# One decoder layer on one core: quads for the last depth tiles of the down projection, and helper work placed elsewhere

## The chip, the cores and the metric

The kernel runs on 1 core of one Trainium2 chip. The metric is the device time of one execution in microseconds (us); lower is better. Three runs of the kernel before took 3001.31, 3004.3 and 3009.29 us, median 3004.3.

## The reference

The program is one inference step of a decoder layer in float32, for 2048 prompt positions and 64 sample positions (8 sequences of 8), with a model width of 1024:

```
h     = rms_norm(x, pre_mix_g);  z = h @ w_in           # q, k, v, sg_u, sg_v, mem-q, 3 x 1024 gate logits
attn  = sliding-window attention (128, 8 q heads, 2 kv heads, sinks, rotary)
sg    = gelu(sg_u) * (tril(sg_w) @ layer_norm(gelu(sg_v)) + sg_b)     # chunks of 128
memo  = 4-head attention into 256 memory tokens
mixed = sum over n of sigmoid(gate_n) * (branch_n @ w_o[n])           # 3 branches of width 512
x     = x + rms_norm(mixed, post_mix_g)
up    = rms_norm(x, pre_ffn_g) @ w_up                   # 1024 -> 2 x 2816
c     = causal convolution of width 3 over up, per channel
x     = x + rms_norm((gelu(c_gate) * c_val) @ w_down, post_ffn_g)     # 2816 -> 1024
```

It also returns the new window keys and values, the memory keys and values, the last spatial-gating values and the last two rows of `up`.

## The kernel before

**Tokens and numbers.** All 2112 tokens lie along the free axis, features on the 128 partitions. After the first stage the tokens form three groups of 704 (`T2`), each handled as two halves of 352 columns (`CW`). Float32 operands are split into a high and a low part, the high one by a cast on ScalarE (L76), the low one by a subtraction on VectorE (L77), and each product is three matmuls (`PASSES`).

**Stages.** Stage 1 computes q, k, v, both attentions (pass A), and then the spatial gating (pass B), with a pool of 5 weight buffers `w1`. Then follow the gate phase (three groups of 12 jobs), the mix phase (output projection, gating and the sum of the branches), the up phase (three groups of 22 jobs, with the convolution), and the down phase.

**Seven products instead of eight.** Class `Strassen` (L761) multiplies a pair of output tiles by two halves of a group with seven products. `operands` (L771) loads 8 depth tiles of the activations, scales them where a norm is due (L780), forms four differences (L790) and splits everything into seven operand sets of four tiles (`HK` = 4). `weights` (L813) gives seven weight tiles: three are splits of raw blocks (`r_...`, loaded at L821), four are sums. In the first group of the gate phase the sums are formed on the spot; elsewhere they were formed ahead of time by `prep_sums` (L103), which loads four raw blocks, adds and splits them, and writes them to `sum_d`. A product is 4 depth tiles x 3 passes = 12 matmuls (L882) into a PSUM bank: x (3 of them), y or w (2 each).

**Gate phase.** The x loads `x_h` and their scaling stand at its start, in pool `ldg`.

**Mix phase.** For each group, branch n and pair op, 48 matmuls (L1023) go to two banks; VectorE multiplies by the gate (L1032, L1035), GpSimd adds (L1036). `post_mix` (L988) of a group is called as a whole once the next group has reached n = 0, op = 1: sum of squares over the partitions (L88), reciprocal root (VectorE L92, GpSimd L95), broadcast by an identity matmul (L98), copy, then for eight tiles a scaling (VectorE L1000), an addition of the input (GpSimd L1003), an output and a square.

**Up phase.** `jobs` (L1190) yields the 22 jobs of a group, 84 matmuls each, and calls helpers between them: `prep_sums` for one tile of `w4s` (the down weights) after f = 3, 7, 11, 15, 19 of the first group and f = 3, 7, 11 of the second; `late` (the last group's residual) at f = 2 to 9 of the first group; `norms` of the next group after f = 14. Raw blocks share a pool of 5 (`rawf`), weight tiles one of 11 (`wof`).

**Down phase.** Per group, two blocks of eight depth tiles by `quad` (L1223), four quads each; then the last six depth tiles by `plain` (L1260): 8 output tiles x 2 halves x 18 matmuls (L1279). The squares for the norm are taken in `plain`. `final` (L1295) of a group is called after the first quad of the next group: statistics as above for each half (tile `ps_sd`), eight scalings (L1306), additions of x1 (loads L1304 into two buffers; L1310) and outputs (L1311). The sums y lie in a pool of 10; a group needs 8. In the last group `plain` and `final` run half by half.

**Order.** The kernel is built under `TileContext(nc, schedule_with_timeline_sim=True)`: the program text gives the work and its dependences, and the scheduler sets each engine's order. All loads and stores are issued by one queue, SP, in its order.

Of the kernel before, what the change touches and what calls it, by code (L numbers as in the profile page):

```python
# [15 lines left out]
P = 128  # L16
# [27 lines left out]
def tile_decoder_layer(ctx, tc, I, O):  # L44
# [9 lines left out]
    sum_d = [dpool.tile([4, P, 2, 512], F32, tag=f"sumd{f}", name=f"sum_d{f}") for f in range(NF + 20)]  # L54
# [48 lines left out]
    def prep_sums(rw, wo, w, sums, nm):  # L103


        def block(i):
            t = rw.tile([P, 512], F32, tag="raw", name=f"r{i}_{nm}")
            nc.sync.dma_start(out=t, in_=w[:, i * 512 : (i + 1) * 512])
            return t

        def total(i, p, m, op):
            t = rw.tile([P, 512], F32, tag="raw", name=f"s{i}_{nm}")
            nc.vector.tensor_tensor(out=t, in0=p, in1=m, op=op)
            r = wo.tile([P, 2, 512], F32R, tag="w", name=f"ws{i}_{nm}")
            split(r[:, 0], r[:, 1], t)
            nc.sync.dma_start(out=sums[i], in_=_f(r))
            return t
# [13 lines left out]
def stage1(tc, I, O, br, rbc_d, mhalf, gains, split, PASSES, rstd_rows, ident, ident_r, prep_sums, sum_d):  # L131
    nc = tc.nc
    PSUM = bass.MemoryType.PSUM
    with ExitStack() as c1:
        wp = c1.enter_context(tc.tile_pool(name="w1", bufs=5))
        hp = c1.enter_context(tc.tile_pool(name="h1", bufs=3))
        st = c1.enter_context(tc.tile_pool(name="st1", bufs=3))
        lv = c1.enter_context(tc.tile_pool(name="live1", bufs=2))
        small = c1.enter_context(tc.tile_pool(name="small", bufs=2))
# [4 lines left out]
        def load_w1(u, stage=None, before=None):  # L144
            w = wp.tile([P, 2, KT * 256], F32R, tag="w", name=f"w1_{u}")
# [116 lines left out]
def pass_a(items, a):  # L262
# [42 lines left out]
    w_a = [load_w1(4 + u, stage) for u in range(5)]  # L305
# [440 lines left out]
def stage2(tc, I, O, br, rbc_d, x1_d, acx_d, act_d, sum_d, sg_d, gains, split, PASSES, rstd_rows, prep_sums, m_d, acm_d):  # L746
# [14 lines left out]
    class Strassen:  # L761
# [9 lines left out]
        def operands(self, xs, nm, gain, rb):  # L771
# [21 lines left out]
            J = range(HK)  # L793
# [6 lines left out]
            for j in J:  # L800
                load(j + HK)
                put("b21", j, chunk(x[j + HK], 0))
            for j in J:
                put("t2", j, sub(t[j], chunk(x[j + HK], 1), t[j]))
            for j in J:
                put("b22", j, chunk(x[j + HK], 1))
            for j in J:
                put("t3", j, sub(chunk(x[j], 1), chunk(x[j + HK], 1), chunk(x[j], 1)))
            for j in J:
                put("t4", j, sub(t[j], chunk(x[j + HK], 0), t[j]))  # L810
            return ops

        def weights(self, w, sums, first, nm):  # L813

            _, _, wo, rw, _, _ = self.pools
            raw = {}

            def block(i):
                if i not in raw:
                    raw[i] = rw.tile([P, HK * P], F32, tag="raw", name=f"r{i}_{nm}")  # L820
                    nc.sync.dma_start(out=raw[i], in_=w[:, i * 512 : (i + 1) * 512])  # L821
# [51 lines left out]
        def product(self, q, bank, w, o, start):  # L873
# [5 lines left out]
            ps, n = banks[bank], 0  # L879
            for j in range(HK):  # L880
                for a, b in PASSES:
                    nc.tensor.matmul(  # L882
                        ps[:, :CW], lhsT=ws[w][:, a, j], rhs=ops[o][j][:, b],
                        start=(start and n == 0), stop=(n == 3 * HK - 1), skip_group_check=True,
# [19 lines left out]
def gate_phase(c2, tc, env):  # L904
# [42 lines left out]
def mix_phase(c2, tc, env):  # L947
# [12 lines left out]
    bc, sp, wp, gp, me = (pool(c2, nm, n) for nm, n in (("bc", 4), ("s2", 2), ("w2", 3), ("sg2", 5), ("mxe", 8)))  # L960
# [510 lines left out]
```

## Time and profile before

| | |
|---|---|
| median of three runs | 3004.3 us |
| profiled execution, its span | 3005.72 us, 3003.9 us |
| mean granted TensorE clock | 0.977 |
| TensorE busy | 2876.0 us, 96% of the span, 19340 instructions |
| VectorE busy | 2064.8 us, 69% |
| ScalarE, GpSimd busy | 1397.5 us (47%), 488.3 us (16%) |
| DMA queue q1 | 728.97 MB, 69.9% of 16 engines |

Busy time is given per engine; the span is the time from the first to the last instruction. The granted clock is the share of full speed that TensorE had, 1.00 for 2.4 GHz. A wait in the profile is the idle time of an engine just before an instruction, with the instruction or transfer that ended it.

### The profile page before, as it was taken

How to read it: one execution, taken by the hardware profiler on the slowest of the kernel's cores; microseconds unless marked ns; L12 is line 12 of the kernel's file. 1: busy time of each engine (PE TensorE's matmuls, PEld its weight loads, DVE VectorE, ACT ScalarE, POOL GpSimd, SP SyncE). 2: the span in 40 equal slices, each digit the busy share in tenths (PEclk: the TensorE clock that was granted, in tenths of full speed). 3: DMA queues.
4: the chain of work that ended last, by engine and by line, in shares of the span. 5: the costliest groups of instructions: out<-in, count | busy, mean ns of one | idle time of the engine just before them, and what ended most of it. 6: DMA issues, size and time to landing. Idle time of an engine off the chain costs nothing. (4 is left out here: it accounts for less than half of the span.)

```text
span 3003.9 us, 52626 instructions
## 1 busy us (share of the span) xinstructions
PE 2876.0 (96%) x19340; PEld 2829.2 (94%) x19340; DVE 2064.8 (69%) x3901; ACT 1397.5 (47%) x2799; POOL 488.3 (16%) x576
## 2 busy tenths in 40 slices
PE   8999999996999999999999899999999999999996
PEld 8998999996999999999989899999999999999996
DVE  6676567888867363478798677766775667667665
ACT  5555557333555353432235355644554454343332
POOL 3221100010000000035453121311231121000000
PEclk9999999998999999999999899999999999999998
DMA  6222224787989999867669788887777778576673
GB/s 209 53 69 85 76 68 126 258 303 248 328 296 371 332 356 346 320 212 264 212 249 364 291 304 310 319 288 278 246 277 247 240 238 279 196 273 223 233 246 119
DMA packets 310946, 732.33 MB, mean 244 GB/s; under 512 B 37968, under 2 KB 90192, under 8 KB 310672
## 3 DMA queue, kind: packets, MB, share of 16 engines
q1 hardware_dynamic: 310688, 728.97, 69.9%
q8 instruction: 153, 2.51, 0.3%
q14 instruction: 105, 0.86, 0.1%
HBM read 553.55 MB, written 176.27 MB: 243 GB/s over the span
## 5 line engine op out<-in xcount | busy, mean ns | idle before, releaser
L1023 PE MATMUL ps_p<-b,w_p 128*128 128x352 f32 x1728 | 287.2, 328 | 13.3 <-DVE m L1032 8.8
L1023 PEld LDWEIGHTS ps_p<-b,w_p 128*128 128x128 f32 x1728 | 283.3, 192 | 15.1 <-issue 10.2
L1165 DVE SCALAR_TENSOR_TENSOR c<-e,k_conv_w,c 128x704 f32<-128x704 f32 (+1 forms) x264 | 251.6, 954 | 43.3 <-ACT c L1161 36.0
L882 PE MATMUL ps_xu<-ot_u,ws_u 128*128 128x352 f32 x1584 | 274.9, 322 | 0.0
L882 PEld LDWEIGHTS ps_xu<-ot_u,ws_u 128*128 128x128 f32 x1584 | 257.1, 188 | 0.0
L1036 POOL TENSOR_TENSOR m<-m,sl 128x704 f32<-128x704 f32 x48 | 101.4, 2119 | 658.0 <-DVE sl L1035 651.8
L77 DVE TENSOR_TENSOR wa_u<-r_u,wa_u 128x512 fp32r<-128x512 f32 x198 | 138.6, 703 | 48.0 <-ACT wa_u L76 43.9
L1161 ACT ACTIVATE c<-e,k_conv_b,k_conv_w 128x704 f32<-128x704 f32 (+1 forms) x132 | 129.6, 981 | 78.6 <-DVE e L1140 43.5
L882 PE MATMUL ps_xu<-ob_u,wa_u 128*128 128x352 f32 x792 | 149.0, 325 | 9.7 <-ACT wa_u L76 9.7
L1152 POOL COPY tails<-e 128x2 f32<-128x2 f32 x88 | 79.2, 900 | 470.0 <-DVE e L1140 469.6
L882 PE MATMUL ps_xg<-ot_h,ws_g 128*128 128x352 f32 x864 | 151.1, 323 | 1.7 <-ACT ws_g L76 0.8
L882 PE MATMUL ps_wu<-ob_u,wa_u 128*128 128x352 f32 x792 | 147.0, 324 | 1.1 <-DVE ob_u L77 1.1
L882 PE MATMUL ps_yu<-ot_u,ws_u 128*128 128x352 f32 x792 | 143.2, 325 | 3.8 <-DVE sl L1035 2.2
L76 ACT CAST wa_u<-r_u 128x512 fp32r<-128x512 f32 x198 | 123.1, 623 | 47.1 <-PE ps_xu L882 15.7
L882 PEld LDWEIGHTS ps_xg<-ot_h,ws_g 128*128 128x128 f32 x864 | 140.6, 188 | 2.4 <-ACT ws_g L76 1.3
L882 PEld LDWEIGHTS ps_xu<-ob_u,wa_u 128*128 128x128 f32 x792 | 131.7, 190 | 9.9 <-ACT wa_u L76 9.9
L1279 PE MATMUL ps_p<-a,wd 128*128 128x352 f32 x864 | 140.1, 323 | 0.0
L1279 PEld LDWEIGHTS ps_p<-a,wd 128*128 128x128 f32 x864 | 138.4, 188 | 0.1
L882 PE MATMUL ps_xu<-ot_u,wa_u 128*128 128x352 f32 x792 | 138.0, 323 | 0.0
L882 PE MATMUL ps_yu<-ob_u,ws_u 128*128 128x352 f32 x792 | 137.7, 323 | 0.0
L882 PEld LDWEIGHTS ps_yu<-ot_u,ws_u 128*128 128x128 f32 x792 | 130.9, 190 | 4.6 <-DVE sl L1035 2.5
L1140 DVE TENSOR_TENSOR e<-p_u,ps_wu 128x352 f32<-128x352 f32 x66 | 34.3, 519 | 145.1 <-PE ps_wu L882 140.3
(381 smaller groups left out, 6786.2 us busy)
## 6 DMA issues: line engine op xcount, KB each, us to landing
ws_u<-sum_d SPq DMA_DIRECT2D x264, 512.0 KB, 4.9
r_u<-in_w_dram SPq DMA_DIRECT2D x286, 256.0 KB, 4.7
ws_g<-sum_d SPq DMA_DIRECT2D x96, 512.0 KB, 8.5
ws_d<-sum_d SPq DMA_DIRECT2D x96, 512.0 KB, 5.1
sum_d<-ws_u SPq DMA_DIRECT2D x88, 512.0 KB, 4.2
r_g<-in_wg_dram SPq DMA_DIRECT2D x120, 256.0 KB, 5.3
r_d<-in_w4s_dram SPq DMA_DIRECT2D x104, 256.0 KB, 4.4
sg_d<-sg SPq DMA_DIRECT2D x72, 352.0 KB, 5.0
```

The source lines that it names most:

```text
L76: nc.scalar.copy(out=hi, in_=src)
L77: nc.vector.tensor_tensor(out=lo, in0=src, in1=_f(hi), op=ALU.subtract)
L882: nc.tensor.matmul(ps[:, :CW], lhsT=ws[w][:, a, j], rhs=ops[o][j][:, b], start=(start and n == 0), stop=(n == 3 * HK - 1), skip_group_chec ...
L1023: nc.tensor.matmul(ps[:, c, :CW], lhsT=w[:, a, 4 * oo + k], rhs=bs[k][:, b, c * CW : (c + 1) * CW], start=(i == 0), stop=(i == 11),)
L1036: nc.gpsimd.tensor_tensor(out=mx[o], in0=mx[o], in1=sg, op=ALU.add)
L1140: lambda out, part: nc.vector.tensor_tensor(out=out, in0=part(p), in1=part(q), op=ALU.add), h, c
L1152: nc.gpsimd.tensor_copy(out=tails[:, ft], in_=e[:, T2 : T2 + 2])
L1161: nc.scalar.activation(c[:, :cwid], e[:, 2:ew], AF.Identity, bias=cb[:, ft : ft + 1], scale=cw[:, ft, 2:3])
L1165: nc.vector.scalar_tensor_tensor(out=c[:, :cwid], in0=e[:, t : t + cwid], scalar=cw[:, ft, t : t + 1], in1=c[:, :cwid], op0=ALU.mult, op1= ...
L1279: nc.tensor.matmul(ps[:, :CW], lhsT=w[k // 4][:, a, k % 4], rhs=acts[k][c][:, b], start=(n == 0), stop=(n == 3 * ND - 1),)
```

## The change

1. **Down phase.** A third block of quads with three depth tiles in each half (`hk` = 3) replaces `plain` in the first two groups. Its weights come from a new input `w4t`, 384 columns to a block, and their sums from four more `prep_sums` (`wide` = 384). Squares are taken in the third block (`done`), and a quad's last product runs into the next group's first quad. The last group is as before.
2. **Up phase.** `prep_sums` is called twelve times, after f = 11 and 14 of the first group, 2, 5, 8, 11, 14 of the second and 1, 4, 7, 10, 13 of the third. `norms` stands after f = 18. `wof` has 10 buffers.
3. **Stage 1 and gate phase.** The pool `w1` has 4 buffers, and one weight of pass A has a buffer of its own. In pass B a tile `free1b` keeps a place of the size of `ldg` free, so that the gate phase's x sources can be loaded and scaled early. The gate and mix pools are opened in another order.
4. **Mix phase.** `post_mix` is a generator: the statistics, then two output tiles at a step, one step after each (n, op) of the next group.
5. **`final`.** The x1 loads have 4 buffers, in the last group 8 in the pool `ldf`.

```diff
@@ prep_sums
-    def prep_sums(rw, wo, w, sums, nm):
+    def prep_sums(rw, wo, w, sums, nm, wide=512):
...
-            nc.sync.dma_start(out=t, in_=w[:, i * 512 : (i + 1) * 512])
-            return t
+            nc.sync.dma_start(out=t[:, :wide], in_=w[:, i * wide : (i + 1) * wide])
+            return t[:, :wide]
@@ stage1
-        wp = c1.enter_context(tc.tile_pool(name="w1", bufs=5))
+        wp = c1.enter_context(tc.tile_pool(name="w1", bufs=4))
...
+            wx = c2.enter_context(tc.tile_pool(name="w1x", bufs=1, side="right"))
...
+            free = c2.enter_context(tc.tile_pool(name="free1b", bufs=1, side="right", reuse_waits="tile"))
+            free.tile([P, 11 * T2], F32, tag="free", name="free1b")
@@ Strassen.product
-            for j in range(HK):
+            for j in range(hk):
@@ mix_phase, post_mix
         acx = xp.tile([P, T2], F32, tag="ax", name=f"acx_{g}")
+        yield
         for o in range(KT):
...
             square(acx, m, o == 0, f"x{g}_{o}")
+            if o % 2:
+                yield
...
-                if held and n == 0 and op == 1:
-                    post_mix(*held)
-                    held = None
-        held = g, mx, acc
+                if held and (n, op) > (0, 0):
+                    next(held, None)
+        held = post_mix(g, mx, acc)
@@ up_phase, jobs
+        preps = [(g, f) for g, fs in ((0, (11, 14)), (1, (2, 5, 8, 11, 14)), (2, (1, 4, 7, 10, 13))) for f in fs]
...
-                if f % 4 == 3 and 5 * g + f // 4 < 8:
-                    i = 5 * g + f // 4
-                    prep_sums(rw, wo, I["w4s"][i], sum_d[NF + 12 + i], f"d{i}")
+                if (g, f) in preps:
+                    i = preps.index((g, f))
+                    w = I["w4s"][i] if i < 8 else I["w4t"][i - 8]
+                    prep_sums(rw, wo, w, sum_d[NF + 12 + i], f"d{i}", 512 if i < 8 else 384)
...
-                if f == 14 and g + 1 < NG2:
+                if f == 18 and g + 1 < NG2:
@@ down_phase
+        done(0)
         add(1, 1, eng.product(q, "x", "s3", "t3", False))
-        return lambda: put(1, 0, eng.product(q, "x", "a22", "t4", False))
+
+        def last():
+            put(1, 0, eng.product(q, "x", "a22", "t4", False))
+            done(1)
+
+        return last
...
-            x = sp.tile([P, T2], F32, tag="x", name=f"xf_{g}_{o}_{c0}", bufs=2)
+            if g + 1 == NG2:
+                x = lp.tile([P, T2], F32, tag="ld", name=f"xf_{g}_{o}_{c0}", bufs=8)
+            else:
+                x = sp.tile([P, T2], F32, tag="x", name=f"xf_{g}_{o}_{c0}", bufs=4)
...
-        for b in range(NB):
-            ops = eng.operands(lambda k: act_d[8 * b + k][:, g * T2 : (g + 1) * T2], f"d{g}_{b}", None, None)
+        for b in range(NB + (g + 1 < NG2)):
+            hk = (HK, HK, ND // 2)[b]
+            ops = eng.operands(
+                lambda k: act_d[8 * b + k][:, g * T2 : (g + 1) * T2], f"d{g}_{b}", None, None, hk
+            )
...
+                end = quad(nm, ws, ops, two, b == 0, end, *((done,) if b == NB else ()))
                 if held:
                     final(*held)
                     held = None
+                    acc = sp.tile([P, T2], F32, tag="acc", name=f"acc_{g}", bufs=1)
-        acts = load_acts(g)
...
         if g + 1 < NG2:
-            plain(g, acts, ys, (0, 1), acc, end)
-            held, end = (g, ys, acc, (0, 1)), None
+            held = g, ys, acc, (0, 1)
```

**Where the order moves, 1: TensorE in the first group of the up phase.** `ps_su_1` is the second half's statistics for the next group's norm; `ps_xu_7` is a bank of job 7. Before:

```order
L882 MATMUL ps_xu_7_18938<-ot_u_3_17844,wa_u_7_18931 128x352 x3
L88 MATMUL ps_su_1_20133<-ones,acx_20118 88x1 x4
L98 MATMUL ps_su_1_20133<-ident,rstd_u_1_20138 128x88 x4
L882 MATMUL ps_xu_8_19118<-ob_u_0_17722,wa_u_8_19093 128x352 x2
L882 MATMUL ps_wu_8_19170<-ob_u_0_17766,wa_u_8_19100 128x352 x2
```

Now:

```order
L88 MATMUL ps_su_1_20670<-ones,acx_20655 88x1 x4
L885 MATMUL ps_xu_19_20708<-ob_u_0_17735,wa_u_19_20683 128x352 x3
L885 MATMUL ps_xu_18_20540<-ot_u_0_17829,ws_u_18_20531 128x352 x3
...
L885 MATMUL ps_yu_19_20745<-ot_u_2_17768,ws_u_19_20688 128x352 x3
L885 MATMUL ps_yu_19_20745<-ot_u_3_17773,ws_u_19_20688 128x352 x2
L98 MATMUL ps_su_1_20670<-ident,rstd_u_1_20675 128x88 x4
```

The pair has moved from between jobs 7 and 8 to jobs 18 and 19, and 35 matmuls (the rows left out are eight of three) stand between its two parts.

**2: VectorE behind `post_mix`'s statistics of the first group.** `rs` is the broadcast root, `m_0` to `m_7` are the eight tiles that are scaled; the `m_5` with `ps_p_0_5` is a product of the next group. Before:

```order
L1032 TENSOR_TENSOR m_4_16037<-sl_0_4_16035,ps_p_0_4_16010 128x704
L994 COPY rs_15939<-ps_st_15919 128x704
L1000 SCALAR_TENSOR_TENSOR m_0_14986<-m_0_14986,c_gains,rs_15939 128x704
...
L1000 SCALAR_TENSOR_TENSOR m_7_15204<-m_7_15204,c_gains,rs_15939 128x704
L1032 TENSOR_TENSOR m_5_16066<-sl_0_5_16064,ps_p_0_5_16039 128x704
```

Now:

```order
L1038 TENSOR_TENSOR m_4_15987<-sl_0_4_15985,ps_p_0_4_15960 128x704
L997 COPY rs_15952<-ps_st_15932 128x704
L1004 SCALAR_TENSOR_TENSOR m_0_14999<-m_0_14999,c_gains,rs_15952 128x704
...
L1004 SCALAR_TENSOR_TENSOR m_7_15217<-m_7_15217,c_gains,rs_15952 128x704
L1038 TENSOR_TENSOR m_5_16016<-sl_0_5_16014,ps_p_0_5_15989 128x704
```

Nothing has moved: the scalings of `m_1` to `m_6` are the rows left out in both.

**3: TensorE at the start of the second down group.** `ps_sd_1` is the statistics of the first group's second half; `ps_xd_0_1`, `ps_wd_0_2` and `ps_xd_0_3` are banks of the second group's quads 1, 2 and 3. Before:

```order
L98 MATMUL ps_sd_1_29761<-ident,rstd_d_1_29766 128x88 x4
L882 MATMUL ps_yd_0_2_29985<-ot_d_0_2_29553,ws_d_0_2_29940 128x352 x2
L882 MATMUL ps_yd_0_2_29985<-ot_d_0_3_29558,ws_d_0_2_29940 128x352 x3
L882 MATMUL ps_wd_0_2_29999<-ob_d_0_0_29563,wa_d_0_2_29942 128x352 x3
...
L882 MATMUL ps_xd_0_3_30077<-ob_d_0_3_29538,wa_d_0_3_30054 128x352 x3
L882 MATMUL ps_xd_0_1_29839<-ot_d_0_0_29582,ws_d_0_1_29828 128x352 x3
```

Now:

```order
L885 MATMUL ps_xd_0_3_30245<-ob_d_0_3_29692,wa_d_0_3_30222 128x352 x3
L88 MATMUL ps_sd_1_29928<-ones,acc_28007 88x1 x4
L98 MATMUL ps_sd_1_29928<-ident,rstd_d_1_29933 128x88 x4
L885 MATMUL ps_xd_0_1_30007<-ot_d_0_0_29736,ws_d_0_1_29996 128x352 x3
L885 MATMUL ps_xd_0_1_30007<-ot_d_0_1_29740,ws_d_0_1_29996 128x352 x3
```

The products of `ps_wd_0_2` and `ps_xd_0_3`, which stood behind L98, now stand ahead of L88, and L98 follows L88 directly.

## Rows read from the trace of the kernel before

**Rows 1.** The page's parts 1 and 5: busy time, share; a group's busy time, mean ns.

```profile
PE 2876.0 (96%) x19340; PEld 2829.2 (94%) x19340; DVE 2064.8 (69%) x3901; ACT 1397.5 (47%) x2799; POOL 488.3 (16%) x576
...
L1279 PE MATMUL ps_p<-a,wd 128*128 128x352 f32 x864 | 140.1, 323 | 0.0
```

**Rows 2.** What TensorE waits for: us in total, times, longest.

```profile
PE ps_xg L882 <- ACT wa_g L76: 19.1, 2, 17.0
PE ps_xd L882 <- ACT y L1229: 17.5, 3, 6.8
PE ps_xu L882 <- ACT wa_u L76: 9.7, 1, 9.7
PE ps_p L1023 <- DVE m L1032: 8.8, 2, 4.4
```

**Rows 3.** Windows of 50 us: busy us and instructions per engine, granted clock, DMA.

```profile
1650.00:1700.00 50.00, 36.32 (x216) 35.51 (x215) 40.72 (x62) 17.68 (x30) 11.73 (x13) 0.81 0.77 283
1700.00:1750.00 50.00, 50.00 (x307) 49.76 (x307) 31.05 (x46) 24.72 (x44) 10.37 (x14) 0.98 0.82 292
2600.00:2650.00 50.00, 50.00 (x314) 50.00 (x313) 37.61 (x76) 22.93 (x46) 0.00 (x0) 1.00 0.57 191
```

**Rows 4.** Timeline of the up phase: start, us, instruction, idle before.

```profile
1683.90 6.12 DVE L780 SCALAR_TENSOR_TENSOR x_u<-x_u,c_gains,rb 128x704 f32<-128x704 f32 x7
1684.38 7.03 SPq L821 DMA_DIRECT2D r_u<-in_w_dram  x3
...
1690.37 0.69 DVE L113 TENSOR_TENSOR s_d<-r_d,s_d 128x512 f32<-128x512 f32 x1
...
1692.28 0.95 PE L882 MATMUL ps_xu<-ob_u,wa_u 128*128 128x352 f32 x2 [9.66 <-ACT wa_u L76]
```

**Rows 5.** Timeline of post_mix of the first group.

```profile
1371.73 12.81 DVE L1000 SCALAR_TENSOR_TENSOR m<-m,c_gains,rs 128x704 f32<-128x704 f32 x8
...
1385.48 14.75 PE L1023 MATMUL ps_p<-b,w_p 128*128 128x352 f32 x75 [4.44 <-DVE m L1032]
```

**Rows 6.** Timeline at the start of the gate phase.

```profile
723.58 1.06 PE L732 MATMUL psg<-sgwb,vg 128*128 128x128 f32 x8
...
737.35 1.82 DVE L77 TENSOR_TENSOR ob_h<-x_h,ob_h 128x352 fp32r<-128x352 f32 x4
...
744.14 1.50 SPq L821 DMA_DIRECT2D r_g<-in_wg_dram  x3
...
748.80 0.95 PE L882 MATMUL ps_xg<-ob_h,wa_g 128*128 128x352 f32 x2 [16.95 <-ACT wa_g L76]
```

**Rows 7.** Timeline at the start of the second down group.

```profile
2660.87 0.71 PE L88 MATMUL ps_sd<-ones,acc 128*88 128x1 f32 x8
...
2661.93 1.00 POOL L95 TENSOR_TENSOR rstd_d<-rstd_d,mhalf 88x4 f32<-88x4 f32 x1 [7.14 <-DVE rstd_d L92]
...
2665.86 1.02 PE L98 MATMUL ps_sd<-ident,rstd_d 88*128 88x88 f32 x8
...
2677.86 0.45 ACT L1229 COPY y<-ps_xd 128x352 f32<-128x352 f32 x1 [5.77 <-DMA out_yT_dram<-y]
...
2678.36 3.48 PE L882 MATMUL ps_xd<-ot_d,ws_d 128*128 128x352 f32 x12 [6.80 <-ACT y L1229]
```

**Rows 8.** Timeline of the end: scalings alone, and with GpSimd beside them.

```profile
2961.41 4.06 DVE L1306 SCALAR_TENSOR_TENSOR y<-y,c_gains,rs_d 128x352 f32<-128x352 f32 x8
...
2982.24 4.72 DVE L1306 SCALAR_TENSOR_TENSOR y<-y,c_gains,rs_d 128x352 f32<-128x352 f32 x8
2983.40 1.20 POOL L1310 TENSOR_TENSOR y<-y,xf 128x352 f32<-128x352 f32 x1 [3.82 <-DVE y L1306]
...
2986.89 1.11 DVE L1310 TENSOR_TENSOR y<-y,xf 128x352 f32<-128x352 f32 x2
...
2996.25 0.94 DVE L1310 TENSOR_TENSOR y<-y,xf 128x352 f32<-128x352 f32 x1 [3.52 <-DMA xf<-x_d]
...
3001.20 0.33 SPq L1311 DMA_DIRECT2D out_yT_dram<-y  x1
```

More of the change, by code (lines that the diff above doesn't have):

```diff
@@ L53, in tile_decoder_layer @@
     acx_d = [dpool.tile([P, T2], F32, tag=f"acxd{g}", name=f"acx_d{g}") for g in range(NG2)]
-    sum_d = [dpool.tile([4, P, 2, 512], F32, tag=f"sumd{f}", name=f"sum_d{f}") for f in range(NF + 20)]
+    sum_d = [dpool.tile([4, P, 2, 512], F32, tag=f"sumd{f}", name=f"sum_d{f}") for f in range(NF + 24)]
     sg_d = [dpool.tile([P, NTOK], F32, tag=f"sgd{i}", name=f"sg_d{i}") for i in range(24)]
@@ L142, in stage1, with load_w1 @@
         ps_tr = c1.enter_context(tc.tile_pool(name="ps_tr", bufs=2, space=PSUM))
-        def load_w1(u, stage=None, before=None):
-            w = wp.tile([P, 2, KT * 256], F32R, tag="w", name=f"w1_{u}")
+        def load_w1(u, stage=None, before=None, pool=None):
+            w = (pool or wp).tile([P, 2, KT * 256], F32R, tag="w", name=f"w1_{u}")
             for i in range(2):
@@ L304, in pass_a @@
     rb_mem, r_mem = rstd_of(x_mem, NMEM, "mem")
-    w_a = [load_w1(4 + u, stage) for u in range(5)]
+    w_a = [load_w1(4 + u, stage, pool=None if u else a["wx"]) for u in range(5)]
     band = kload("band", [P, 256])
@@ L769, in __init__, with operands @@
             self.pools = ps, op_, wo, rw, cp, lp
-        def operands(self, xs, nm, gain, rb):
+        def operands(self, xs, nm, gain, rb, hk=HK):
             _, op_, _, _, _, lp = self.pools
@@ L791, in sub @@
                 return out
-            J = range(HK)
+            J = range(hk)
             for j in J:
@@ L883, in product @@
                         ps[:, :CW], lhsT=ws[w][:, a, j], rhs=ops[o][j][:, b],
-                        start=(start and n == 0), stop=(n == 3 * HK - 1), skip_group_check=True,
+                        start=(start and n == 0), stop=(n == 3 * hk - 1), skip_group_check=True,
                     )
@@ L1051, in ffn_phase @@
     env["lp"], env["rw"], env["wo"] = (
-        pool(c2, nm, n, "right") for nm, n in (("ldf", 1), ("rawf", 5), ("wof", 11))
+        pool(c2, nm, n, "right") for nm, n in (("ldf", 1), ("rawf", 5), ("wof", 10))
     )
@@ L1221, in down_phase, with quad @@
     eng = Strassen(ps2, op_, wo, rw, None, lp)
-    def quad(nm, ws, ops, ys, first, end):
+    def quad(nm, ws, ops, ys, first, end, done=lambda o: None):
         q = [nm, ws, ops, None, {}]
@@ L1287, in plain @@
                 nc.vector.tensor_tensor(out=chunk(ys[o], c), in0=chunk(ys[o], c), in1=ps[:, :CW], op=ALU.add)
[L1288 to L1293 removed]
+            squares(acc, ys[o], o, c0, c1, nm)
     def final(g, ys, acc, cs):
@@ L1320, in down_phase, with done @@
                     ys += [yp.tile([P, T2], F32, tag="y", name=f"y_{g}_{2 * op + h}") for h in range(2)]
-                i, nm = 4 * b + op, f"d{g}_{b}_{op}"
-                ws = eng.weights(I["w4s"][i], sum_d[NF + 12 + i], False, nm)
-                end = quad(nm, ws, ops, ys[2 * op : 2 * op + 2], b == 0, end)
+                i, nm, two = 4 * b + op, f"d{g}_{b}_{op}", ys[2 * op : 2 * op + 2]
+                ws = eng.weights(I["w4s"][i] if b < NB else I["w4t"][op], sum_d[NF + 12 + i], False, nm, hk)
+                def done(o, op=op, two=two, acc=acc, nm=nm):
+                    squares(acc, two[o], 2 * op + o, 0, T2, f"{nm}_{o}")
+                end = quad(nm, ws, ops, two, b == 0, end, *((done,) if b == NB else ()))
                 if held:
@@ L1411, in _layout @@
     )
+    r["w4t"] = np.stack(
+        [
+            np.concatenate([dn[2 * op + oo][:, 16:].reshape(P, (NF - 16) * P) for oo in range(2)], 1)
+            for op in range(4)
+        ]
+    )
     r["w4"] = np.stack([dn[o][:, 16:].reshape(P, (NF - 16) * P) for o in range(KT)])
```

60 lines of the change are left out of this document (31 added, 29 removed).

## The prediction

> **What bounds the kernel now.** I read the page first, then the list of what TensorE waits for, then 50-us windows, and then the timeline around each long wait. TensorE is busy for 2876.0 of 3003.9 us [rows 1], so it is the bound almost everywhere, and a change is worth either the matmuls that it removes or the idle stretches that it closes; a faster helper engine alone brings nothing. A stretch without waits holds 314 matmuls of 352 columns in 50 us, 0.16 us each, at a granted clock of 1.00, which is the 2.4 GHz level (the window from 2600 us) [rows 3]. The idle stretches are few. The largest single one, 17.0 us, stands ahead of the gate phase; three before ps_xd sum to 17.5, one in the up phase is 9.7, and two before ps_p are 4.4 each [rows 2]. Each costs more than its idle time, because the matmuls behind it run slower: the 12 behind the 6.80 us wait took 3.48 us instead of 1.92 [rows 7], and the window of the up-phase wait has a granted clock of 0.81, a mixture of the two levels, 1.2 and 2.4 GHz [rows 3]. At the very end TensorE is done while VectorE, GpSimd and the queue still work for 20 us [rows 8].
>
> **The change part by part.** Each part is set against the profiled execution, 3005.72 us, 1.4 us above the median of 3004.3.
>
> *Fewer matmuls.* The plain product of the last six depth tiles is 864 matmuls, 288 per group [rows 1]. In two groups it becomes four quads of 7 products x 3 depth tiles x 3 passes = 63, so 252. That is 2 x 36 = 72 matmuls less, x 0.16 = **-11.5 us**. They lie on TensorE's path with no wait around them [rows 3], so this is a full gain, if the quads keep pace.
>
> *Do they keep pace?* Plain, VectorE is busy 37.61 of 50 us [rows 3], or 34.7 us over a group's 46.1 us of matmuls. In the quads the next group's operands are the same; from the code I count 32 additions into y instead of 16, and 12 narrower weight splits instead of 16, at about half a microsecond each, some 5 us more, and 40.3 us of matmuls: 39.7 of 40.3. Every add or split that comes late holds a PSUM bank or a weight. I take +2 us per group, **+4 us**, with 0 and +8 as the ends.
>
> *Up phase, first group.* The two statistics of the next group's norm stand back to back, and with them come seven scalings in a row (6.12 us), in front of the sums of a w4s tile (s_d at 1690.37). The raw-weight buffers are held by those sums, so the queue takes 7.03 us to issue three r_u loads, and TensorE waits 9.66 us for wa_u [rows 4]. Moving norms from f = 14 to f = 18, and the sums to f = 11 and 14, takes both away from each other: in the new order 35 matmuls, 5.6 us, stand between L88 and L98 of the second statistics, and from L88 to the end of the step on GpSimd the same chain took 2.06 us in the down phase [rows 7]; three weights ahead are already split when the scalings begin, and no sums are near. The two windows hold 216 and 307 matmuls against 314 [rows 3], so (98 + 7) x 0.16 = **-16.8 us** is there to be had. The eight scalings and four subtractions, some 9 us of VectorE, now hide behind the matmuls of a job, 84 x 0.16 = 13.4 us. If that cover fails, the stall comes back: the term lies between -16.8 and 0. I take all of it. The four new sums in the second and third group land in windows where VectorE has a third of its time free; I cost them at nothing, and at 4 us if they meet the scalings.
>
> *post_mix stepped.* VectorE runs the eight scalings in 12.81 us, and TensorE waits 4.44 us behind them, twice, and then runs 75 matmuls in 14.75 instead of 12.0 [rows 5]. The generator should spread them. But the scheduler has set them in the same place as before: copy, eight scalings, then the product's m_5, in both groups. I cost it at **0**; -14, both stalls with their slow matmuls, is out of reach in that order, and a shift of some loads behind the scalings may move it by 2 either way.
>
> *Early gate sources.* The first group's x_h loads and scalings go to the start of pass B. What TensorE waits for is wa_g, cast from r_g, and r_g is issued at 744.14 [rows 6]. In the new order the r_g loads stand behind a load of the second group's first x_h, whose buffer comes free with the first t3 split. From the end of the psg matmuls at 724.6 I count 29 VectorE instructions of 352 columns up to that split, 0.455 each [rows 6], and 11 of 512, 0.69 each [rows 4]: 20.8 us, so 745, the same within 1 us. **0**, from -6 (had the queue gone on) to +4 (a second weight then split later).
>
> *Boundaries between the down groups.* The second group's y_2 needs the buffer of the first group's y_0, which is free once its output is written: TensorE's next product waits 6.80 us [rows 7]. This stays. The chain from L88 at 2660.87 to the restart at 2678.36 is 17.49 us, and before it has 9 us of matmuls inside (56 x 0.16). In the new order these are all issued ahead: L88, L98 and then the waiting product, nothing between. L98 need no longer queue behind other matmuls (POOL is done at 2662.93, L98 ran at 2665.86), which shortens the chain by 2.9 us to 14.6; 1.7 of it is L88 and L98, and 12.9 is idle against 6.8. With 1.4 us more at the low clock, +7.5 per boundary, twice: **+15 us**, from 0 (if TensorE arrives there late anyway) to +20.
>
> *The last group's x1 loads.* At the end, additions wait for loads that wait for buffers, two by two: from the scalings at 2982.24 to the last output at 3001.20 is 18.96 us [rows 8]. With eight buffers all loads are issued before the scalings start. Left are the scalings, four additions on VectorE at 0.55 (two took 1.11) and the issue, 0.4. Eight scalings took 4.06 us alone and 4.72 with one GpSimd addition beside them [rows 8]; with three beside, 4.06 + 3 x 0.66 = 6.0. So 6.0 + 2.2 + 0.4 = 8.6, a gain of **-10.4 us**, from -12.5 (no disturbance) to -4 (some loads still late). The Trainium skill, "SBUF — State Buffer", section "SBUF: two separate sides", speaks against more than that: VectorE with two SBUF inputs and GpSimd take the shared port pair in turn, each for a whole instruction. By that rule the three additions, 1.20 each [rows 8], would cost in full, 7.7 instead of 6.0, and the term would be -8.7; the row at 2982.24 shows half of it, so I stay with the row.
>
> *Fourth w1 buffer less, one wof buffer less.* A weight of the up phase has 9 products or more, 17 us, from its buffer's release to its use. 0, with 4 either way at the start of pass B.
>
> Sum: -11.5 + 4 - 16.8 + 0 + 0 + 15 - 10.4 = -19.7, so 3005.7 - 19.7 = 2986.0, or 2984.6 against the median. I say **2985 us**.
>
> **The rivals.** A difference under 0.3%, 9 us, can't be told from none here: 2995 to 3013.
>
> *A, the boundaries cost nothing new.* For it: TensorE loses the same chain either way if VectorE's additions and splits, 39.7 of 40.3 us, make it arrive late. Against it: the new order has nothing behind L98. Then 2984.6 - 15 - 4 = 2965.6. Chance 0.12.
>
> *B, the up-phase stall moves and does not go.* For it: all eight scalings still stand in a row, and wa_u of jobs 20 and 21 stand behind them. Against it: they are needed a job later. Then 2984.6 + 16.8 = 3001, the same. Chance 0.16.
>
> *C, slower: the narrow quads starve on VectorE.* One place, the two third blocks; mechanism: at 39.7 of 40.3 us every wait is handed on to the next bank, and TensorE between such waits drops to the low level, where 12 matmuls took 3.48 us (0.29 each), 0.13 more than before. With half of the 504 matmuls there, 252 x 0.13 = 33 us, 3017. It decides from about 14 us lost per group on; there the whole forecast gain and 9 us more are gone. Against it: with the plain product VectorE is at three quarters of its time and TensorE waits nowhere [rows 3], and part of the operands' subtractions can be done a block earlier. Chance 0.07.
>
> *D, the forecast,* stepping and early sources without effect: 0.65, own range 2972 to 2995.
>
> **How the numbers follow.** Faster: A, D except the few cases past 2995 (0.04 of 0.65), so 0.12 + 0.61 = 0.73. Same: B and those few, 0.20 with rounding. Slower: C, 0.07. The range goes from 2969, in the middle of A, to 3001, B's own number: outside lie half of A, C and a part of B's upper half, near 0.2.
>
> **What would show it.** ps_p's group with the last six depth tiles has 288 matmuls left, all in the last group. No wait near the tenth job of the up phase. The two 4.4 us waits behind post_mix's scalings stand as before, and so does the wait ahead of the gate phase, 15 to 19 us. Two waits of ps_xd behind y's copy of 12 to 14 us, in place of 6.8. From the last scalings to the last output 8 to 9 us. The forecast is wrong if the boundary waits are near 7, if the up stall returns at jobs 19 to 21, or if TensorE shows many short waits for VectorE in the third blocks.

## The result, and the profile after

The changed kernel took 2981.5 us (median of four runs, 2978.1 to 2983.4), the kernel before 3002.8 beside it: a ratio of 0.9924 (95% interval 0.9908 to 0.9940), 21 us less. 2985 had been said. The profiled execution took 2978.08 us, span 2976.3, 27.6 less than the profiled one of before; since both lie off their medians, on opposite sides, some 6 us of that is scatter.

Where the 27.6 us lie, by the first and last matmuls of each stage's products in the two timelines (the tail holds the last statistics, too):

| stretch | before | after | difference | forecast |
|---|---|---|---|---|
| start to the gate's first product | 748.8 | 737.6 | -11.2 | 0 |
| gate phase | 505.1 | 509.8 | +4.7 | 0 |
| mix, to the first up product | 307.7 | 304.5 | -3.2 | 0 |
| up phase | 927.3 | 917.0 | -10.3 | -16.8 |
| down, last up product to last down product | 485.6 | 488.3 | +2.7 | +7.5 |
| tail, to the end of the span | 29.4 | 19.2 | -10.2 | -10.4 |

What TensorE waits for now (us in total, times, longest), against [rows 2]:

```profile
PE ps_xd L885 <- ACT y L1236: 24.0, 3, 11.5
PE ps_xg L885 <- ACT wa_g L76: 19.9, 2, 18.2
PE ps_p L1029 <- DVE m L1038: 9.1, 2, 4.6
...
PE psg L735 <- DVE ob L739: 5.9, 1, 5.9
PE ps_sd L98 <- POOL rstd_d L95: 5.1, 3, 1.8
```

The up phase's wait for wa_u is gone; the two before post_mix's products stand unchanged, the one ahead of the gate phase is 1.3 longer, and ps_xd's has grown. Windows of 50 us (PE, PEld, DVE, ACT, POOL, then granted clock, DMA share, GB/s), against [rows 3]:

```profile
1650.00:1700.00 50.00, 50.00 (x317) 49.99 (x317) 33.57 (x48) 24.68 (x42) 11.63 (x17) 1.00 0.89 330
1800.00:1850.00 50.00, 50.00 (x321) 49.99 (x320) 41.53 (x65) 25.30 (x47) 11.94 (x17) 1.00 0.70 235
2150.00:2200.00 50.00, 46.70 (x289) 45.85 (x288) 47.37 (x90) 31.21 (x62) 31.14 (x23) 1.00 0.79 282
2650.00:2700.00 50.00, 41.09 (x246) 41.09 (x247) 38.91 (x73) 19.81 (x44) 0.00 (x0) 0.87 0.82 304
2750.00:2800.00 50.00, 50.00 (x314) 50.00 (x313) 44.31 (x91) 23.87 (x47) 0.00 (x0) 1.00 0.90 301
```

At 1650 us there are 317 matmuls in place of 216, and at 1800 us, where the next group's scalings now stand, 321. At 2150 us, where the third up group begins and a preparation of sums stands after its second job, there are 289, where its neighbours hold 312 to 316; two waits stand there:

```profile
2189.84 0.59 PE L885 MATMUL ps_wu<-ob_u,wa_u 128*128 128x352 f32 x2 [1.35 <-ACT wa_u L76]
...
2193.44 2.16 PE L885 MATMUL ps_yu<-ot_u,ws_u 128*128 128x352 f32 x12 [1.41 <-DMA ws_u<-sum_d]
```

At 2750 us, in a third block of quads, VectorE is at 44 of 50 and TensorE waits for nothing: the quads keep pace. At 2650 us lies a boundary between down groups; its timeline (start, us, instruction, idle before), against [rows 7]:

```profile
2643.75 0.71 PE L88 MATMUL ps_sd<-ones,acc 128*88 128x1 f32 x8
...
2646.29 1.12 PE L98 MATMUL ps_sd<-ident,rstd_d 88*128 88x88 f32 x8 [1.82 <-POOL rstd_d L95]
...
2648.01 6.99 DVE L1325 SCALAR_TENSOR_TENSOR y<-y,c_gains,rs_d 128x704 f32<-128x704 f32 x8
2654.91 3.29 DVE L1329 TENSOR_TENSOR y<-y,xf 128x704 f32<-128x704 f32 x4
2655.83 0.34 SPq L1330 DMA_DIRECT2D out_yT_dram<-y  x1
...
2658.40 0.45 ACT L1236 COPY y<-ps_xd 128x352 f32<-128x352 f32 x1 [13.45 <-DMA out_yT_dram<-y]
...
2658.91 3.89 PE L885 MATMUL ps_xd<-ot_d,ws_d 128*128 128x352 f32 x12 [11.50 <-ACT y L1236]
```

TensorE stands for 1.82 + 11.50 = 13.3 us, and most of that is VectorE: y_0 is scaled first, but its addition stands behind all eight scalings (6.99 us). The end, against [rows 8]:

```profile
2964.26 6.06 DVE L1325 SCALAR_TENSOR_TENSOR y<-y,c_gains,rs_d 128x352 f32<-128x352 f32 x8
2965.42 1.20 POOL L1329 TENSOR_TENSOR y<-y,xf 128x352 f32<-128x352 f32 x1 [3.82 <-DVE y L1325]
2966.65 7.10 SPq L1330 DMA_DIRECT2D out_yT_dram<-y  x8
...
2970.25 2.55 DVE L1329 TENSOR_TENSOR y<-y,xf 128x352 f32<-128x352 f32 x4
```

No wait for a load is left, and the last output is issued within 9.5 us of the first scaling. Mix and gate, against [rows 5, 6]:

```profile
732.91 0.33 SPq L781 DMA_DIRECT2D x_h<-in_xT_dram  x1
...
733.30 1.37 SPq L824 DMA_DIRECT2D r_g<-in_wg_dram  x3
...
737.64 0.95 PE L885 MATMUL ps_xg<-ob_h,wa_g 128*128 128x352 f32 x2 [18.21 <-ACT wa_g L76]
...
1366.03 12.78 DVE L1004 SCALAR_TENSOR_TENSOR m<-m,c_gains,rs 128x704 f32<-128x704 f32 x8
...
1379.75 2.69 PE L1029 MATMUL ps_p<-b,w_p 128*128 128x352 f32 x8 [4.52 <-DVE m L1038]
```

The weights r_g leave right behind the second group's x_h, as the order had it, and the scalings are as long as before (12.81).

### The profile page after: what moved, and what is told of

The parts are those of the page before. It is cut to its first block, busy times and chain, and to the rows that moved or that the text cites. A ratio compares the mean times of both kernels' runs of the same rounds, so it can differ in the third digit from the quotient of the medians.

```text
span 2976.3 us, 52703 instructions
## 1 busy us (share of the span) xinstructions
PE 2856.3 (96%) x19268; PEld 2808.2 (94%) x19268; DVE 2096.1 (70%) x3991; ACT 1408.1 (47%) x2819; POOL 502.6 (17%) x576
## 4 chain that ended last, share of the span: by engine, by line
PE 85%; DVE 5%; DMA 5%; issue 2%; ACT 2%; POOL 1%; SPq 0%; DVEq 0%; ACTq 0%; POOLq 0%
PE ps_xu L885 17%; PE ps_xg L885 9%; PE ps_yu L885 8%; PE ps_p L1029 8%; PE ps_xd L885 8%; PE ps_yg L885 5%; PE ps_wu L885 4%; PE ps_yd L885 4%; PE ps_mqp L229 3%; PE ps_q L215 3%; PE ps_wg L885 2%; PE ps_wd L885 2%; PE ps_kv L215 2%; PE ps_sv L215 2%; PE ps_up L229 1%
## 5 line engine op out<-in xcount | busy, mean ns | idle before, releaser
L885 PE MATMUL ps_xd<-ot_d,ws_d 128*128 128x352 f32 x720 | 129.4, 329 | 24.0 <-ACT y L1236 24.0
L1157 POOL COPY tails<-e 128x2 f32<-128x2 f32 x88 | 73.2, 832 | 460.4 <-DVE e L1145 450.3
L885 PEld LDWEIGHTS ps_xd<-ot_d,ws_d 128*128 128x128 f32 x720 | 120.0, 193 | 24.7 <-ACT y L1236 24.7
L885 PEld LDWEIGHTS ps_wu<-ob_u,wa_u 128*128 128x128 f32 x792 | 131.3, 190 | 1.9 <-ACT wa_u L76 1.9
```

The costliest lines, as they stand in the source:

```text
L885: nc.tensor.matmul(ps[:, :CW], lhsT=ws[w][:, a, j], rhs=ops[o][j][:, b], start=(start and n == 0), stop=(n == 3 * hk - 1), skip_group_chec ...
L1157: nc.gpsimd.tensor_copy(out=tails[:, ft], in_=e[:, T2 : T2 + 2])
```

## Experiments

Twelve kernels ran, each with the kernel before on the same chip (medians 3003.7 to 3005.4 us).

| kernel | median us (lowest to highest) | ratio to before, 95% interval |
|---|---|---|
| changed, old places in the up phase | 3000.9 (2996.9 to 3007.1) | 0.9992 [0.9984, 1.0001] |
| changed, old stage 1 and gate | 2982.7 (2978.2 to 2986.2) | 0.9930 [0.9918, 0.9942] |
| changed, plain product | 2981.8 (2974.2 to 2985.8) | 0.9926 [0.9914, 0.9938] |
| changed, old x1 buffers | 2994.4 (2988.6 to 2996.4) | 0.9966 [0.9954, 0.9979] |
| 12 y buffers | 2962.6 (2961.3 to 2968.2) | 0.9869 [0.9854, 0.9883] |
| 12 y buffers, plain | 2960.5 (2958.0 to 2962.8) | 0.9858 [0.9843, 0.9873] |
| 12 y buffers, scalings held apart | 2966.9 (2964.0 to 2975.6) | 0.9882 [0.9867, 0.9897] |
| 12 y buffers, f = 12, 13 in the gate | 2955.4 (2949.9 to 2957.5) | 0.9836 [0.9823, 0.9849] |
| new placement, plain | 2933.0 (2925.0 to 2935.2) | 0.9756 [0.9742, 0.9771] |
| new placement, quads, 15 y buffers | **2924.3** (2923.5 to 2927.9) | 0.9735 [0.9721, 0.9748] |
| the same, additions on GpSimd | 2939.8 (2936.8 to 2945.5) | 0.9790 [0.9777, 0.9804] |
| the same, two more sums moved | 2941.1 (2936.0 to 2942.6) | 0.9781 [0.9767, 0.9795] |

### Parts undone

**Up phase.**

```diff
-((0, (11, 14)), (1, (2, 5, 8, 11, 14)), (2, (1, 4, 7, 10, 13)))
+((0, (3, 7, 11, 15, 19)), (1, (3, 7, 11, 15, 19)), (2, (3, 7)))
-                if f == 18 and g + 1 < NG2:
+                if f == 14 and g + 1 < NG2:
```

> The changed kernel with the up phase's part undone: norms after f = 14 again, and the twelve preparations of sums in the old raster, after f = 3, 7, 11, 15, 19. The changed kernel stands at 2981.5 us. Theory of the prediction: the 9.7 us wait near the tenth job of the first up group comes back whole with its slow matmuls, +16.8, 2998. Second theory, from the two traces: from the first to the last up matmul only 10.3 us went, because the five preparations of the third group take some back (two waits of 1.4 us at its second job); then the stall comes back and those waits go, +10, 2992. Rival: other parts of the change took the stall away (buffers, order), so nothing comes back, 2980 to 2984.

The first theory's number came (2998 said, 3000.9 measured), and its wait, in the timeline of this kernel:

```profile
1691.28 0.95 PE L885 MATMUL ps_xu<-ob_u,wa_u 128*128 128x352 f32 x2 [12.38 <-ACT wa_u L76]
```

But of the 19.4 us only 15.0 lie in the up phase (932.0 against 917.0); the down phase, whose order changed too, takes 5.6 more. Split at every 1848 matmuls, the up phase shows where (us per group of tokens):

| kernel | first group | second | third |
|---|---|---|---|
| before | 324.7 | 299.1 | 303.5 |
| changed | 309.1 | 299.3 | 308.6 |
| changed, old places | 329.8 | 299.1 | 303.1 |

The stall was worth 15.6 us, near the 16.8 said. What hides it in the total is the third group, 5.1 longer in the changed kernel. It is not the number of sums: in the old raster the second and third groups have two more each than before and take no longer, and the changed kernel's second group has five for three; a kernel further down has six in the third group and takes 303.1. What the changed kernel's third group alone has is a sum after its second job, f = 1, with the two short waits shown above. The first group of this kernel is 5.1 longer than before's with the same five sums; one weight buffer less and the order are not told apart there.

**Stage 1 and gate.** The gate and mix pools are opened in the old order too.

```diff
-        wp = c1.enter_context(tc.tile_pool(name="w1", bufs=4))
+        wp = c1.enter_context(tc.tile_pool(name="w1", bufs=5))
...
-            wx = c2.enter_context(tc.tile_pool(name="w1x", bufs=1, side="right"))
...
-            free.tile([P, 11 * T2], F32, tag="free", name="free1b")
```

> The changed kernel with stage 1's and the gate phase's part undone: w1 has 5 buffers, no extra weight buffer, no place kept free for early sources, gate and mix pools in the old order. Theory: the 12.4 us by which the last psg matmuls came earlier (717.35 instead of 729.77) are this part's work, although I had put it at 0; undone, psg ends near 730 again, of which the gate phase gives 4.7 back, so +6.5, 2988, and up to 2992. Rival: the 12.4 us are scatter between two executions (granted clock at the start of pass B); then psg ends at 717 to 720 here too, and the time stays at 2979 to 2984.

Mixed. The last psg matmuls end at 729.8 here, against 719.4, and between 717 and 724 in the six other runs with the same pass B: the gain is this part's work, no scatter. Some 6 of the 10.4 us are there at the first psg matmuls already (531.7 against 525.8). In the pass the short waits for h_bp are back. But the medians differ by 1.2 us only, inside the runs' spread; by the two profiled executions 4.6 reach the end of the up phase. What the part is worth, 1 to 5, stays open.

**Plain product for the quads.**

```diff
-        for b in range(NB + (g + 1 < NG2)):
+        for b in range(NB):
...
+            plain(g, acts, ys, (0, 1), acc, end)
+            held, end = (g, ys, acc, (0, 1)), None
```

> The changed kernel with the plain product of the last six depth tiles in all three groups again; the other parts stay, the four added preparations too. 72 matmuls come back, +11.5. Theory, from the traces: the two boundaries fall back from 13.3 us of idle time to about 6.8, with fewer slow matmuls behind them, -13 to -15, so the quads as they stand bring nothing: 2979, between 2976 and 2982. Prediction's terms taken alone (11.5 - 4 - 15 = -7.5): 2974. Rival: the boundary waits don't come from the quads and stay at 13 us; then +11.5, 2993.

As the traces' theory said: 2981.8, so in the changed kernel 72 fewer matmuls bring nothing. Each of its boundaries has 5.3 us of wait for wa_d and 1.0 for y, in place of 13.3.

**x1 buffers.**

```diff
-            if g + 1 == NG2:
-                x = lp.tile([P, T2], F32, tag="ld", name=f"xf_{g}_{o}_{c0}", bufs=8)
-            else:
-                x = sp.tile([P, T2], F32, tag="x", name=f"xf_{g}_{o}_{c0}", bufs=4)
+            x = sp.tile([P, T2], F32, tag="x", name=f"xf_{g}_{o}_{c0}", bufs=2)
```

> The changed kernel with the x1 loads of final as before: two buffers in every group. Theory (the term of the prediction): from the last eight scalings to the last output 19 us again instead of 9, so +10.4, 2992; the boundary waits of the first two groups stay at 11.5, since y_0's output doesn't need a third load. Rival: with eight loads in flight at the end the additions still wait, and the whole gain at the end came from the shorter statistics: then +3, 2984.

+12.9 by the medians; the scalings start at 2970.86 and the last output is issued at 2989.34, 18.5 us. The theory holds, 2.5 us stronger.

### The boundary

```diff
-    yp, sp = pool(c2, "yd", 10), pool(c2, "sd", 1)
+    yp, sp = pool(c2, "yd", 12), pool(c2, "sd", 1)
...
-                x = sp.tile([P, T2], F32, tag="x", name=f"xf_{g}_{o}_{c0}", bufs=4)
+                x = sp.tile([P, T2], F32, tag="x", name=f"xf_{g}_{o}_{c0}", bufs=2)
```

> The changed kernel with 12 instead of 10 buffers for y in the down phase, paid for with 2 instead of 4 buffers for the x1 loads of the first two groups. Theory: the wait at a boundary is for the buffer of y_0 alone; with two more buffers the second quad of a group (13.4 us of matmuls) runs while the first outputs leave, so both waits of 11.5 us go, and their slow matmuls: -2 x 12.5, 2957, between 2954 and 2962. Rival: the wait moves on to the third quad, because with two x1 buffers the outputs of y_0 and y_1 leave later than 13 us after L88: half comes back, 2969. Second rival: TensorE is held by L98's wait for GpSimd (1.8 us) and by VectorE anyway, and only a third goes: 2973.

-18.9 of the -25 said. At the first boundary of this kernel the waits are shorter and later:

```profile
2660.75 0.43 PE L885 MATMUL ps_xd<-ob_d,wa_d 128*128 128x352 f32 x1 [1.64 <-DVE ob_d L77]
...
2664.55 3.89 PE L885 MATMUL ps_xd<-ot_d,ws_d 128*128 128x352 f32 x12 [3.37 <-ACT y L1236]
```

So it lies between theory and first rival: the wait moved on to the third quad and shrank.

**With the plain product** in addition, by the same edit as above:

> The kernel with 12 buffers for y (2962.6 us), with the plain product of the last six depth tiles in all three groups. It tells what the quads are worth once no buffer of y holds the boundary. Theory: 72 matmuls x 0.16 = +11.5, and the plain form's boundary had its own wait for y and a weight (5.3 us), which goes with the buffers too: 2974, between 2971 and 2977. Rival 1: the quads are worth nothing even then (their additions keep VectorE as late as the matmuls saved): 2963. Rival 2: with plain, the two buffers bring nothing, since its statistics had more matmuls beside them: 2982.

My theory failed: plain is not 11.5 us slower (2.2 faster, with overlapping ranges). With 12 buffers the plain form has no wait beyond 0.6 us at a boundary, the quads keep 2 x (3.4 + 1.6) and slow matmuls: that still eats the 72.

### Work around the waits

**Scalings held apart.** `post_mix` scales into a tile of its own with two buffers.

```diff
+            s = xp.tile([P, T2], F32, tag="sm", name=f"sm_{g}_{o}", bufs=2)
...
-            nc.gpsimd.tensor_tensor(out=m, in0=m, in1=x, op=ALU.add)
+            nc.gpsimd.tensor_tensor(out=m, in0=s, in1=x, op=ALU.add)
```

> The kernel with 12 buffers for y (2962.6 us), and post_mix's scaling writes to a tile of its own with two buffers, which GpSimd's addition frees; so the scheduler can't set eight scalings in a row any more: in the order two stand ahead of m_5, two behind it, and the rest one by one between products. Theory: the two waits of 4.5 us for m_5 go, with the slow matmuls behind them, -14 as worked out before the run: 2949, between 2947 and 2955. Rival: the scalings themselves were not the wait; VectorE is short by the same time spread over the next jobs, and half comes back: 2956.

Refuted. Both waits for m_5 are gone, yet the up phase starts only 0.7 us earlier. TensorE ran ahead and then stood in a window where VectorE has no time left (columns as above, this kernel first, then the one with the scalings in a row):

```profile
1500.00:1550.00 50.00, 42.64 (x253) 41.26 (x252) 48.02 (x54) 13.97 (x22) 26.24 (x12) 0.97 0.60 209
```

```profile
1500.00:1550.00 50.00, 46.97 (x294) 46.11 (x294) 48.04 (x54) 16.18 (x25) 28.69 (x13) 1.00 0.63 224
```

As I read it, the stall was the price of VectorE work due anyway before the up phase's first operands. The +4.3 in the total lies in the down phase (477.1 against 471.8), whose order differs too.

**Two sums out of pass B.**

```diff
-NF1 = 14
+NF1 = 12
...
-                if g and i % 3 == 0:
+                if g and i % 5 in (0, 2):
```

> The kernel with 12 buffers for y (2962.6 us), with the sums of two up weights (f = 12 and 13) formed in the gate phase instead of at the end of pass B. In the order the gate's first weight loads then stand right behind the last of these stores, ahead of pass B's last two outputs, and all r_g of the first two jobs are split before x_h is done. Theory: the 18 us wait ahead of the gate phase was for VectorE's and the queue's work on f = 12 and 13 (16 VectorE instructions of 0.69, 11 us, and eight stores), not for the x sources; it falls to 5 or less, -13 with the slow matmuls behind it, 2950. Rival: the first products then wait for the x_h splits, 28 VectorE instructions, as long as before: 2961. The ten sums in the gate phase cost under 2 us there.

The theory on the start holds: the gate's first product comes at 717.3 instead of 737.1, with 1.75 us of wait. But the gate phase ends only 8.5 earlier, and 7.2 of the 13 us said came in all; from 900 us on TensorE waits for weights (wa_g, 8.7 us) and for ScalarE's copies of products (u_g, 9.0), with the DMA nearly full:

```profile
900.00:950.00 50.00, 48.75 (x302) 48.17 (x301) 24.21 (x41) 18.54 (x36) 0.00 (x0) 1.00 1.00 381
...
1100.00:1150.00 50.00, 43.44 (x250) 42.25 (x249) 19.95 (x33) 20.66 (x40) 0.00 (x0) 0.93 0.98 360
```

That the DMA is the cause is not shown: without these two sums the first window holds 312 matmuls at a DMA share of 0.99.

### Put together

The sums of f = 12 and 13 are formed in the gate phase, f = 20 and 21 in the first up group; the sums of the down weights follow from the second group on, after f = 2, 5, 8, 11, 14 and, in the third, 4, 8, 12. The down phase is plain, with 12 y buffers.

```diff
-NF1 = 14
+NF1 = 12
...
-        todo = list(range(NF1, NF))
+        todo = list(range(NF1, NF - 2))
...
+                if g == 0 and f in (11, 14):
+                    f1 = NF - 2 + (f == 14)
+                    prep_sums(rw, wo, I["w3"][f1], sum_d[f1], f"u{f1}")
```

> A version put together from the runs: plain last six depth tiles in all groups, 12 buffers for y, the sums of f = 12 and 13 in the gate phase, those of f = 20 and 21 in the first up group (after f = 11 and 14), so the gate phase has its eight sums as before, and only the eight sums of w4s in the up phase. Theory: 2960.5 (plain with 12 buffers) - 7.2 for the gate start - 3 for the two sums that the gate's DMA (0.9 to 1.0 busy from 900 us on) need not carry - 4.7 for the four sums of w4t that are not formed (the up phase with twelve in the old raster was 4.7 longer than with eight): 2946, between 2942 and 2952. Rival: the sums cost nothing where they stand, only the gate start counts: 2953.

13 us better than said: the gate phase takes 506.8 us here against 521.6 with ten sums, so two sums there, and the closer places of all ten, cost 15, not 3. The gate's first group, which has no sums, takes as long in both (170.8 and 169.8). The up phase's third group, without a sum after f = 1, is back at 303.1, so the theory's 4.7 came for that place and not for four sums fewer.

**With the quads,** so with four more sums, after f = 1, 4, 7, 10, 13, 16 of the second group and 2, 5, 8, 11, 14, 17 of the third:

```diff
-    yp, sp = pool(c2, "yd", 10), pool(c2, "sd", 1)
+    yp, sp = pool(c2, "yd", 15), pool(c2, "sd", 1)
...
-                x = sp.tile([P, T2], F32, tag="x", name=f"xf_{g}_{o}_{c0}", bufs=4)
+            x = lp.tile([P, T2], F32, tag="ld", name=f"xf_{g}_{o}_{c0}", bufs=8)
```

> The same placement of sums, with the quads of three depth tiles in the first two groups (so twelve sums in the up phase), and 15 buffers for y, which take the place of final's own x1 and root buffers (these come from the operands' load pool). Theory: the quads lost their 11.5 us to the last y waits (2 x 3.4, and slow matmuls behind them) and to VectorE being late at the boundary (2 x 1.6); with 15 buffers the y waits go, and the quads are worth about 8 over plain, less 4.7 for the four sums: 2943. Rival: VectorE is the limit at the boundary (eight scalings and eight additions of 0.87, 14 us, beside a block's operands), and the waits only change their name to ob_d and wa_d: as plain or slower, 2947 to 2955.

The theory's sign holds, and the quads are worth 8.8 us over plain: the down phase -10.1 (470.8 against 480.9, first down product to last product; 11.5 by the matmuls), the up phase +3.7. The larger pools are not what plain lacked: its boundaries had no wait left to give. The +3.7 lies in the second up group alone (303.0 against 299.3), which has a sum after f = 1 here; the third, with six sums and none there, takes 303.1. So four more sums are free, and that one place costs, as in the changed kernel; the kernel without it was not run. At the boundary TensorE hardly stops any more:

```profile
2650.00:2700.00 50.00, 49.19 (x306) 48.59 (x305) 42.86 (x95) 20.69 (x43) 0.00 (x0) 1.00 0.87 311
```

**Additions on GpSimd:**

```diff
-            e = nc.gpsimd if o % 2 and g + 1 == NG2 and cs[-1] else nc.vector
+            e = nc.gpsimd if g + 1 < NG2 or (o % 2 and cs[-1]) else nc.vector
```

> As the kernel with quads and 15 buffers, and final's additions of x1 in the first two groups on GpSimd, which does nothing there, instead of VectorE: 2 x 8 x 0.89 = 14 us of VectorE less. Theory, if VectorE is the limit at the boundary: 3 to 6 us less than with the additions on VectorE, 2939 where that is 2943. Rival: beside a GpSimd addition VectorE's instructions get longer (post_mix's scalings took 12.81 for eight with GpSimd beside them, final's 6.99), so VectorE wins nothing: the same within 2 us, or 4 slower.

Worse than its rival: +15.5. Eight scalings of final, alone in the kernel with the additions on VectorE, and with GpSimd beside them:

```profile
2623.24 6.99 DVE L1325 SCALAR_TENSOR_TENSOR y<-y,c_gains,rs_d 128x704 f32<-128x704 f32 x8
```

```profile
2622.38 15.69 DVE L1325 SCALAR_TENSOR_TENSOR y<-y,c_gains,rs_d 128x704 f32<-128x704 f32 x8
2623.47 18.20 POOL L1329 TENSOR_TENSOR y<-y,xf 128x704 f32<-128x704 f32 x8 [5.62 <-DVE y L1325]
...
2644.01 1.25 PE L885 MATMUL ps_xd<-ot_d,wa_d 128*128 128x352 f32 x3 [6.81 <-DVE y L1244]
```

VectorE's addition into y stands behind 15.69 us of scalings, and TensorE waits for it, at both boundaries.

**Two more sums moved:**

```diff
-                if g and i % 3 == 0:
+                if g and i % 4 == 0:
...
+                if g == 0 and f in (5, 8, 11, 14):
```

> As the kernel with quads and 15 buffers, with two more sums (f = 18 and 19) moved from the gate phase to the first up group, after f = 5 and 8; six are left in the gate phase, four jobs apart. Theory, if the two waits of 2 us for wa_g that are left in the gate phase are DMA's (0.92 to 0.97 busy there): they go with their slow matmuls, 2924.3 - 6 = 2918. Rival: the gate phase has nothing more to give back, and the first up group, whose DMA is already fully busy from 1600 to 1650 us, pays for the added 3 MB: 2924 to 2932.

Refuted on balance. The gate phase is 7.7 us shorter, but the up phase 19.7 longer, all of it in its first group (329.3 against 309.2): the stall returns. The norm's scalings stand near the tenth job again (1651.6 us), with sums around them.

```profile
1673.59 0.95 PE L885 MATMUL ps_xu<-ob_u,wa_u 128*128 128x352 f32 x2 [6.33 <-ACT wa_u L76]
```

## Why the prediction was right, and where its terms were not

The total came within 4 us, partly because errors cancelled: the up phase gave 6.5 us less than forecast, the way to the gate's first product 11.2 more, of which about half was lost again. The parts undone one by one sum to 33.8 us, more than the 21 measured, because undoing one does not restore the kernel before (its first up group is then 5.1 longer than before's).

- *Fewer matmuls, -11.5, and keeping pace, +4.* The quads keep pace without a wait, so the +4 was not there. The count behind it was wrong, too: a third block has 28 additions into y and not 32 (the down phase's quads have 176 against 120, 56 more for two blocks), and its own operands, 21 splits and 12 subtractions against plain's 12 splits, were left out. VectorE bears both (44 of 50 us). The -11.5 is real only once the boundary is open: -10.1 with 15 buffers.
- *Boundaries, +15.* 13.3 us idle each, 12.9 said, by the chain that was read from before's rows. The three down terms sum to +7.5; +2.7 came, the missing 4.8 being mostly the +4.
- *Up phase, -16.8.* The mechanism was right, and so was the size: the first group gave -15.6, and the stall came back at 12.4 us when the places were undone. The step that failed is the zero for the sums' new places: the one after the third group's second job cost 5.1. The phase as a whole gave -10.3.
- *post_mix, 0.* Right, from the order: scalings in a row, both waits of 4.5 unchanged. That 14 us were to be had there was not borne out: held apart, the scalings gave nothing.
- *Early gate sources, 0.* Right in its reason: the wait ahead of the gate stays, 18.2. The 724.6 that it counts from is not the end of the psg matmuls, of which eight more run until 731.9; but from the same place r_g comes after 21.9 us in the changed kernel, 20.8 said. Not foreseen: that pass B itself would end 10 us earlier. Against the kernel with this part undone, 9.1 us are there at the gate's first product and 4.6 at the end of the up phase.
- *x1 loads, -10.4.* -10.2 in the tail, +12.9 when undone. Scalings with three GpSimd additions beside them took 6.06; 6.0 had been worked out. The rule of the Trainium skill, "SBUF — State Buffer", section "SBUF: two separate sides", has the two engines take the shared ports in turn, each for a whole instruction. The trace agrees with the turns (last section), but the price of one was 0.67 us and not the addition's whole 1.20, so 6.06 and not the 7.7 that had been worked out from it.
- *Rivals.* A fell with the waits of 11.5 us, B with the full windows at 1650 and 1800 us (no wait of TensorE from 1560 to 2180), C with the full window at 2750 us.

## What to carry to other kernels

A saving on the bound engine counts only where the next boundary does not give it back as idle time: here 72 matmuls were worth nothing with 10 or 12 buffers for the sums y, and 10 us with 15 (and eight buffers for the x1 loads; the two are not told apart). Work prepared ahead of time costs what its place is short of: two sums cost 15 us in the gate phase, next to nothing in most places of an up group, 4 to 5 us for one after a group's second job, and a stall beside the norm's scalings. So split a stage before explaining its total. A visible wait need not be the price of the code in front of it: ask where its work goes when it is spread.

## What the hardware showed that was not expected

VectorE's scalings took turns with GpSimd's additions, as the single rows read. In the changed kernel's tail, a scaling that started beside an addition took 1.25 us instead of 0.58 and ended 0.38 us after it, three times of three:

```profile
2965.42 1.20 POOL L1329 TENSOR_TENSOR y<-y,xf 128x352 f32<-128x352 f32 x1 [3.82 <-DVE y L1325]
2965.75 1.25 DVE L1325 SCALAR_TENSOR_TENSOR y<-y,c_gains,rs_d 128x352 f32<-128x352 f32 x1
```

So an addition cost VectorE 0.67 us, and three the 2.0 us between 6.06 and the 4.06 of [rows 8]. The recorded 1.20 is not the price: the last addition of the kernel with the old x1 buffers, alone, took 0.93. At 128x704, in the kernel with the additions on GpSimd, each of six scalings took 2.4 us instead of 0.95 and ended 0.74 after an addition, which makes the 15.69. What mattered was where VectorE's operands lay. In the same kernel an addition into y from a PSUM bank kept its 0.51 us beside GpSimd, while the split next to it, from SBUF alone, took 1.72; with the additions on VectorE the two take 0.50 and 0.68:

```profile
2637.99 0.51 DVE L1244 TENSOR_TENSOR y<-y,ps_wd 128x352 f32<-128x352 f32 x1
2638.42 1.72 DVE L77 TENSOR_TENSOR wa_d<-r_d,wa_d 128x512 fp32r<-128x512 f32 x1
```

```profile
2635.20 0.50 DVE L1244 TENSOR_TENSOR y<-y,ps_yd 128x352 f32<-128x352 f32 x1
...
2636.43 0.68 DVE L77 TENSOR_TENSOR wa_d<-r_d,wa_d 128x512 fp32r<-128x512 f32 x1
```

Moving work from VectorE to an idle GpSimd lengthened VectorE's chain: 14 us of additions were taken off it, and the kernel became 15.5 us slower.
